# A mixture-of-experts stage with the token lists and gathers first, two tensors for its sums, and its overflow branch moved to the front

## The chip, the cores and the metric

The kernel runs as one program on one core of a Trainium2 chip. The metric is the device time of one execution in microseconds (us), the median of several runs. Engines are named as the profile names them: PE (TensorE products, and PEld its weight loads), DVE (VectorE), ACT (ScalarE), POOL (GpSimd), SP (SyncE); a "q" behind a name is that engine's own queue (branches, waits, DMA issues).

## The reference

Two transformer blocks of two layers each run over 512 tokens of width 1024. Each layer of the first block ends in a hierarchical mixture of experts, and this stage is what the change touches; it occurs twice in the program.

```python
glog = einsum('bsd,dg->bsg', x, wg) + bg                 # 4 groups
gp, gi = top_k(softmax(glog), 1)                         # one group for each token
elog = (the 4 expert logits of that group)
ep, ei = top_k(softmax(elog), 2); ep = ep / sum(ep)      # two experts of that group
combine = sum(one_hot(gi * 4 + ei, 16) * (gp * ep))      # [512, 16], two entries a row
h = silu(x @ w_gate[e]) * (x @ w_up[e]) * combine[:, e]  # 16 experts, 1024 -> 256
ffn = sum over e of h @ w_down[e]                        # 256 -> 1024
x = layernorm(ALPHA * x + ffn)
```

A token's two experts always lie in one group of four (experts 0 to 3, 4 to 7, 8 to 11, 12 to 15), so each expert has 512 x 2 / 16 = 64 tokens on average.

## The kernel before

Matrices are float32 in the interface. On the chip each operand is split into a high and a low float16 part (ACT writes the high part at L133 or L143, DVE the low part at L134 or L144), and each product is three float16 products (`mm3`, L146 to L151).

**Tokens to experts.** `moe` (L1128) first makes the router logits (`rlog`) on PE. DVE then picks the group and the two experts (`first_max`), computes the combination weights `cmb`, and from a triangular product (`pos`, L1186) each token's place in its expert's list. An expert has `CAP` = 104 places. `onehots(e0)` (L1208) makes the one-hot matrices of two experts, eight DVE operations; `select` (L1217) makes expert 0's features with 64 products from the rows that are still in SBUF (the four `xrow` tiles, which fill all four buffers of the pool `xg`); `slots` (L1284) multiplies the one-hots with `V` (token number, three parts of the weight, a one) and so gets for each place the token number, whether it is used, and its weight `cw`. For the other experts an indirect DMA on POOL's queue (`gather`, L1316) fetches all 104 rows, 4 KB each, from the DRAM tensor `rows`, an empty place fetching row 0; `feats` (L1303) transposes them on PE, and ACT copies them out (L1312).

**The loop over experts** (L1353) is written out. In round e PE's order is the features of expert e + 2, the first half of `front(e + 1)` (24 groups of gate and up products, L149 to L151, tile `gu`), the two transposes of expert e (`hT`, L1436), the second half of `front(e + 1)`, and `back(e)`, the down products (tile `ey`). For experts 0 to 13, `back` copies the result out (`yt`, L1329, three buffers) and adds it to the DRAM tensor `res` with an accumulating indirect DMA on POOL's queue (L1332) in which places beyond the list are dropped. All 14 of these scatters write the one tensor `res`, so each waits until the one before has landed. The last two experts keep their results in SBUF and are summed by PE (`ysum`, L1398).

**Weights.** An expert's weights are three chunks of 1 MB (gate and up in two halves, down), 48 chunks in a layer. SP issues their loads (L122) into five staging buffers, so the load of chunk c waits for the split of chunk c - 5. `fetch(n)` splits up to chunk n; the split parts go round 12 pairs of buffers, two of which are the former `xT` tiles. Before the loop `fetch` reaches 9; in round 0 it reaches 10, in round e it reaches 3(e + 3) + 1.

**Overflow.** `overflow` (L1448) handles tokens beyond an expert's 104 places. Every engine loads the count `oi` into a register (L1453) and jumps over the body when it is zero (L1454), as it is for these inputs. The body is a loop over experts with the four token tiles written out. It stands in round 14, behind `back(14)` and ahead of `back(15)`.

**The end.** At the end of round 13 four DMAs on POOL's queue read `res` back (`mx`, L1383), after the last scatter has landed. Then each token tile gets its sum on PE (`ysum`, L1398 and L1400) and its layer norm.

## Time and profile before

| | before |
|---|---|
| median of 3 runs | 2452.76 us (2444.24 to 2454.18) |
| the profiled execution | 2442.73 us |
| its span in the trace | 2441.0 us |
| PE, DVE, ACT, POOL busy in the span | 91%, 70%, 47%, 11% |
| the first expert stage, from the router to the sums | about 316 to 536 us |
| the second expert stage | about 843 to 1081 us |

What lies around the span is 1.7 us. Busy PE time in the profile is modelled: two products that overlap in the pipeline both count. In a timeline row the first number is the start, the second the time to the end of the group (xN is how many), and the bracket tells how long the engine had been idle and what the profile takes for the releaser. A wait for several semaphores is put down to the one that came last; where the engine named had long been done it was another, often a DMA.

### The profile page before, as it was taken

Reading aid. Unit: us, or ns where it says so; the run is one execution under the profiler, and the core shown is the slowest. Engines: PE = TensorE matmul, PEld = TensorE weight load, DVE = VectorE, ACT = ScalarE, POOL = GpSimd, SP = SyncE. Lnnn points to the kernel's source line nnn. Section 1 sums busy time; section 2 is a strip of 40 time slices with the busy share of each in tenths; the row PEclk is TensorE's granted clock in tenths of the full one; section 3 lists DMA queues with packets and bytes.
Section 4 is the critical chain, followed back from the end, with each engine's and each line's share of the span. In section 5 each row is a group of like instructions: output and inputs, shape, how many; then the busy total and the mean of one; then the engine's idle time right before and its main releaser. Section 6 shows DMA issues by size and latency. Waiting matters only on the chain.

```text
span 2441.0 us, 34718 instructions
## 1 busy us (share of the span) xinstructions
PE 2218.6 (91%) x13330; PEld 1210.9 (50%) x13334; DVE 1698.7 (70%) x3668; ACT 1149.9 (47%) x1965; POOL 269.9 (11%) x335
## 2 busy tenths in 40 slices
PE   8888969888889878869998899999999989999999
PEld 4545545544546455535455554444444556544444
DVE  7978878778978868768999654442469996544421
ACT  5546637845546547724545443222245455332320
POOL 1221022221310122211100100000000000000000
PEclk9999979999999989979998999999999999999999
DMA  5311559953311659933212242222331112422222
GB/s 184 122 62 43 181 177 310 339 188 105 115 59 61 242 179 335 309 125 120 74 48 81 71 168 104 104 104 80 130 123 61 61 54 83 167 104 104 104 78 78
DMA packets 58976, 319.45 MB, mean 131 GB/s; under 512 B 9908, under 2 KB 10164, under 8 KB 30384
## 3 DMA queue, kind: packets, MB, share of 16 engines
q1 hardware_dynamic: 40448, 263.67, 30.5%
q0 software_dynamic: 13744, 36.68, 5.7%
q10 hardware_dynamic: 4608, 16.78, 1.8%
q8 instruction: 108, 1.77, 0.3%
q14 instruction: 68, 0.56, 0.1%
HBM read 286.59 MB, written 30.90 MB: 130 GB/s over the span
## 4 chain that ended last, share of the span: by engine, by line
PE 39%; DVE 10%; ACT 4%; issue 2%; DMA 1%; DVEq 0%; ACTq 0%
PE fd L149 3%; PE fd L150 3%; PE fd L151 3%; PE fu L151 3%; PE fg L151 3%; PE fu L150 3%; PE fg L150 3%; PE fu L149 3%; PE fg L149 3%; PE o L795 2%; DVE wl L134 1%; PE gqk L149 1%; PE gqk L151 1%; PE gqk L150 1%; DVE mx L1801 1%
## 5 line engine op out<-in xcount | busy, mean ns | idle before, releaser
L134 DVE SCALAR_TENSOR_TENSOR wl<-wst,wh 128x1024 f16<-128x1024 f32 (+1 forms) x428 | 513.3, 1226 | 205.2 <-ACT wh L133 201.2
L133 ACT ACTIVATE wh<-wst 128x1024 f16<-128x1024 f32 (+1 forms) x428 | 430.2, 1047 | 278.0 <-PE fd L151 107.1
L150 PEld LDWEIGHTS <-wh 128*128 128x128 f16 x968 | 95.4, 99 | 101.9 <-issue 3.8
L151 PEld LDWEIGHTS <-wl 128*128 128x128 f16 x968 | 95.7, 99 | 100.8 <-issue 2.2
L149 PEld LDWEIGHTS <-wh 128*128 128x128 f16 x968 | 95.7, 99 | 99.5 <-issue 2.1
L149 PE MATMUL fd<-wh,fhh 128*128 128x512 f16 x352 | 133.4, 379 | 0.0
L150 PE MATMUL fd<-wl,fhh 128*128 128x512 f16 x352 | 133.4, 379 | 0.0
L151 PE MATMUL fd<-wh,fhl 128*128 128x512 f16 x352 | 133.4, 379 | 0.0
L149 PE MATMUL gqk<-wh,xTh 128*128 128x512 f16 x320 | 122.7, 384 | 7.6 <-ACT rsq L1685 7.3
L151 PE MATMUL gqk<-wh,xTl 128*128 128x512 f16 x320 | 122.7, 384 | 0.0
L150 PE MATMUL gqk<-wl,xTh 128*128 128x512 f16 x320 | 122.6, 383 | 0.0
L149 PE MATMUL fg<-xTh,wh 128*128 128x512 f16 x320 | 121.3, 379 | 0.0
L150 PE MATMUL fg<-xTl,wh 128*128 128x512 f16 x320 | 121.3, 379 | 0.0
L151 PE MATMUL fg<-xTh,wl 128*128 128x512 f16 x320 | 121.3, 379 | 0.0
L149 PE MATMUL fu<-xTh,wh 128*128 128x512 f16 x320 | 121.3, 379 | 0.0
L150 PE MATMUL fu<-xTl,wh 128*128 128x512 f16 x320 | 121.3, 379 | 0.0
L151 PE MATMUL fu<-xTh,wl 128*128 128x512 f16 x320 | 121.3, 379 | 0.0
L150 PEld LDWEIGHTS <-xTh 128*128 128x128 f16 x768 | 74.9, 99 | 71.6 <-issue 13.1
L149 PEld LDWEIGHTS <-xTh 128*128 128x128 f16 x768 | 74.9, 99 | 67.8 <-ACT xTh L143 5.2
L151 PEld LDWEIGHTS <-xTl 128*128 128x128 f16 x768 | 74.3, 99 | 65.9 <-DVE xTl L144 4.6
L1860 DVE SCALAR_TENSOR_TENSOR fth<-fth,fg 128x512 f32<-128x512 f32 x40 | 27.5, 687 | 107.5 <-ACT fth L1859 107.5
L149 PE MATMUL gO<-wh,mTh 128*128 128x512 f16 x256 | 97.7, 383 | 1.5 <-ACT mTh L143 1.4
(615 smaller groups left out, 5471.1 us busy)
## 6 DMA issues: line engine op xcount, KB each, us to landing
wst<-in_w_gu SPq DMA_DIRECT2D x108, 1024.0 KB, 6.5
wst<-in_w_dn SPq DMA_DIRECT2D x52, 1024.0 KB, 4.8
wst<-in_w SPq DMA_DIRECT2D x28, 1024.0 KB, 4.9
wst<-in_wB SPq DMA_DIRECT2D x16, 1024.0 KB, 4.9
wst<-in_w_out SPq DMA_DIRECT2D x16, 1024.0 KB
dk<-d_nc SPq DMA_DIRECT2D x16, 512.0 KB, 3.6
res<-xa SPq DMA_DIRECT2D x8, 512.0 KB
rows<-xrow SPq DMA_DIRECT2D x8, 512.0 KB
```

The lines of the kernel that those rows point to most:

```text
L133: nc.scalar.activation(wh[:, a:b], st[:, a:b], AF.Copy, scale=scale)
L134: (eng or nc.vector).scalar_tensor_tensor(wl[:, a:b], st[:, a:b], scale, wh[:, a:b], op0=ALU.mult, op1=ALU.subtract)
L149: mm(out, ah, bh, start=start, stop=False)
L150: mm(out, ah, bl, start=False, stop=False)
L151: mm(out, al, bh, start=False, stop=stop)
L795: mm(out, p[:, bs], v, start=first, stop=last)
L1801: nc.vector.tensor_reduce(mr[:, t, h:h + 1], ps[:, :n], axis=AX.X, op=ALU.max)
L1860: nc.vector.scalar_tensor_tensor(th, th, 1.0, pg, op0=ALU.add, op1=ALU.mult)
```

## The change

The program computes the same function. The parts, in the order of the diff:

1. **Two tensors for the sums.** `res` becomes two DRAM tensors, both set to the residual by `finish` (four more 512 KB writes a layer on SP's queue). Experts are taken in the order `ORD` = 0, 8, 1, 9, ..., 7, 15, so that even rounds (groups 0 and 1) add to `res[0]` and odd rounds to `res[1]`. Reading back, an indirect DMA takes for each token the row of the tensor that its group went to: eight DMAs in place of four, each with the other tensor's tokens out of bounds.
2. **Lists and gathers first.** `pos` is made by one operation, the one-hots follow at once, and `slots` needs only the token number. An empty place gets an index of 1024, and the gather has a bounds check. The gather of expert 1 goes to a zeroed buffer of its own instead of to the pool that holds `xrow`. Combination weights, `V` and the overflow count come behind the gathers of experts 1 to 3.
3. **Weights split sooner.** `fetch` reaches 9 ahead of the combination weights, 10 ahead of the loop, 12 and 13 in round 0, 15 in round 1, 17 in round 2, and from round 3 on what it reached before. The features of expert 2 come behind `front(1)` instead of ahead of it.
4. **The branch.** `overflow` stands ahead of `front(0)`. Its body is a loop over experts and in it a loop over token tiles, with room in the two `xT` tiles, and it adds to both sum tensors.

```diff
+ORD = [8 * (i % 2) + i // 2 for i in range(NEXP)]
...
+            nx["res"] = [self.drg.tile([T, D], F32, name="res%d" % i, bufs=1) for i in range(2)]
...
-            nc.sync.dma_start(nx["res"][t * P:(t + 1) * P], xa)
+            for r in nx["res"]:
+                nc.sync.dma_start(r[t * P:(t + 1) * P], xa)
...
+            xg1 = m2.tile([P, 2 * D], F16, tag="yt", name="xg1", bufs=self.YT)[:CAP]
+            nc.gpsimd.memset(xg1, 0.0)
...
-            nc.vector.tensor_copy(pos, ps[:, :NT * NEXP].rearrange("p (t e) -> p t e", t=NT))
-            inb = mp.tile([P, NT, NEXP], F32, name="inb")
-            nc.vector.scalar_tensor_tensor(inb, pos, float(CAP), msk, op0=ALU.is_lt, op1=ALU.mult)
+            nc.vector.scalar_tensor_tensor(pos, ps[:, :NT * NEXP].rearrange("p (t e) -> p t e", t=NT), 1.0, mskh,
+                                           op0=ALU.add, op1=ALU.mult)
...
-            nc.vector.scalar_tensor_tensor(posm, pos, 1.0, inb, op0=ALU.add, op1=ALU.mult)
-            nc.vector.tensor_scalar(posm, posm, -1.0, None, op0=ALU.add)
...
+                    nc.vector.scalar_tensor_tensor(midx[:, i], hi[:, :, 0], (2048.0, -2048.0)[i], self.tokf[:, i],
+                                                   op0=ALU.mult, op1=ALU.add)
...
-                        nc.tensor.matmul(ps[:CAP, 5 * e:5 * e + 5], ohs[:, t, e], V[:, t, e0 + e],
+                        nc.tensor.matmul(ps[:CAP, e:e + 1], ohs[:, t, e], self.tokh[:, t:t + 1],
                                          start=t == 0, stop=t == 3)
...
+                nc.vector.tensor_scalar(sidx[:CAP, eg], ps[:CAP, :2], 1024.0, None, op0=ALU.add)
...
-                                             in_offset=bass.IndirectOffsetOnAxis(ap=sidx[:CAP, 0, e:e + 1], axis=0))
+                                             in_offset=bass.IndirectOffsetOnAxis(ap=sidx[:CAP, e:e + 1], axis=0),
+                                             bounds_check=T - 1, oob_is_err=False)
...
-                    nc.gpsimd.indirect_dma_start(out=cur["res"], in_=yt, in_offset=None,
-                                                 out_offset=bass.IndirectOffsetOnAxis(ap=sidx[:CAP, 1, e:e + 1], axis=0),
+                    nc.gpsimd.indirect_dma_start(out=cur["res"][e % 2], in_=yt, in_offset=None,
+                                                 out_offset=bass.IndirectOffsetOnAxis(ap=sidx[:CAP, e:e + 1], axis=0),
                                                  bounds_check=T - 1, oob_is_err=False, compute_op=ALU.add)
...
-            last = slots(0, ohs)
             xgs = {}
-            gather(1)
-            slots(2, onehots(2))
-            ps = [p for p in front(0, xt[0])][0]
-            with tc.issue_after(last.ins):
-                fetch(9)
+            xo = [m2.tile([P, KD, P], F16, tag="xgt%d" % i, name="xgo%d" % i) for i in range(2)]
+            ohs = onehots(0)
+            slots(0, ohs)
+            gather(1)
+            xt = [select(ohs, 0)]
+            oh2 = onehots(2)
+            slots(2, oh2)
             gather(2)
             gather(3)
+            fetch(9)
+            weights()
+            beyond()
+            slot_weights(0, ohs)
+            self.tap("cmb%d" % l, cmb)
+            self.overflow(l, m2, oi, cov, xr_d, xo, feats, cur["res"])
+            ps = [p for p in front(0, xt[0])][0]
+            fetch(10)
+            slot_weights(2, oh2)
+            oh4 = onehots(4)
+            slots(4, oh4)
+            slot_weights(4, oh4)
             xt.append(feats(xgs[1]))
-            slots(4, onehots(4))
             ys, mx = [], []
-            fetch(9)
...
-                if e + 2 < NEXP:
+                if 0 < e < NEXP - 2:
                     xt.append(feats(xgs[e + 2]))
...
+                if e == 0:
+                    xt.append(feats(xgs[2]))
+                    fetch(12)
...
-                    fetch(3 * (e + 3) + 1 if e else 10)
-                if e == NEXP - 2:
-                    self.overflow(l, m2, oi, cov, xr_d, feats, mx)
+                    fetch(max(3 * (e + 3) + 1, 13 + 2 * e))
...
-                        x = self.xg.tile([P, D], F32, tag="xg", name="mx")
-                        nc.gpsimd.dma_start(x, cur["res"][t * P:(t + 1) * P])
-                        mx.append(x)
+                        mx.append(self.xg.tile([P, D], F32, tag="xg", name="mx"))
+                    for i in range(2):
+                        for t in range(NT):
+                            nc.gpsimd.indirect_dma_start(out=mx[t], out_offset=None, in_=cur["res"][i],
+                                                         in_offset=bass.IndirectOffsetOnAxis(ap=midx[:, i, t:t + 1], axis=0),
+                                                         bounds_check=T - 1, oob_is_err=False)
...
-                for t, x in enumerate(sums):
+                with tc.For_i(0, NT, 1) as t:
...
+                    for q in sums:
+                        nc.gpsimd.indirect_dma_start(out=q, in_=y, in_offset=None,
+                                                     out_offset=bass.IndirectOffsetOnAxis(ap=ti, axis=0),
+                                                     compute_op=ALU.add)
```

## Rows read from the trace of the kernel before

**Rows 1.** First stage by stretch: PE, PEld, DVE, ACT, POOL, clock, DMA, GB/s

```profile
350.00:360.00 10.00, 6.51 (x41) 4.42 (x39) 2.28 (x17) 3.13 (x4) 1.95 (x2) 0.52 0.76 172
360.00:380.00 20.00, 19.54 (x126) 12.24 (x125) 13.66 (x30) 14.19 (x20) 5.90 (x4) 1.00 0.58 178
...
440.00:460.00 20.00, 15.73 (x99) 9.54 (x98) 15.44 (x27) 15.97 (x22) 4.37 (x3) 1.00 1.01 338
```

**Rows 2.** DMA queues from 410 to 490 us: packets, MB, share of 16 engines

```profile
q1 hardware_dynamic: 3171, 23.10, 80.1%
q0 software_dynamic: 1677, 4.08, 20.6%
```

**Rows 3.** Start times of expert transposes on PE, first stage, then second stage

```profile
360.34 0.34 PE L1436 MATMUL hT<-idf,eth 104*128 104x104 f32 x2
369.39 0.34 PE L1436 MATMUL hT<-idf,eth 104*128 104x104 f32 x2
...
499.18 0.34 PE L1436 MATMUL hT<-idf,eth 104*128 104x104 f32 x2
...
886.92 0.34 PE L1436 MATMUL hT<-idf,eth 104*128 104x104 f32 x2
...
1023.86 0.34 PE L1436 MATMUL hT<-idf,eth 104*128 104x104 f32 x2
```

**Rows 4.** POOL's timeline: first gather, last scatters and read-backs of each stage

```profile
342.64 1.72 POOL L1319 DMA_INDIRECT xg<-rows,sidx  x1 [11.31 <-DVE cwt L1299]
...
504.15 2.47 POOL L1332 DMA_INDIRECT res<-yt,sidx  x1 [3.95 <-ACT yt L1329]
514.23 1.63 POOL L1332 DMA_INDIRECT res<-yt,sidx  x1 [7.61 <-ACT y L143]
520.86 2.27 POOL L1383 DMA_DIRECT2D mx<-res  x4 [5.00 <-DMA res<-yt,sidx]
...
1031.31 1.68 POOL L1332 DMA_INDIRECT res<-yt,sidx  x1 [3.66 <-ACT yt L1329]
1044.89 2.66 POOL L1332 DMA_INDIRECT res<-yt,sidx  x1 [11.90 <-ACT wh L133]
1055.95 2.24 POOL L1383 DMA_DIRECT2D mx<-res  x4 [8.41 <-DMA res<-yt,sidx]
```

**Rows 5.** Timeline of ACT and PE: expert 13 copied out, first product with `mx`

```profile
504.92 0.62 ACT L1329 ACTIVATE yt<-ey 104x512 f32<-104x512 f32 x1
...
527.08 2.08 PE L1400 MATMUL ysum<-mx,ida 128*128 128x512 f32 x2 [4.15 <-DMA mx<-res]
...
1029.95 0.63 ACT L1329 ACTIVATE yt<-ey 104x512 f32<-104x512 f32 x1
...
1059.89 2.07 PE L1400 MATMUL ysum<-mx,ida 128*128 128x512 f32 x2 [9.18 <-DMA mx<-res]
```

**Rows 6.** Timeline of DVE at the head of the first stage: one-hots, indices

```profile
335.74 0.39 DVE L1213 TENSOR_SCALAR ohs<-iota_h,posm 128x104 f16<-128x104 f16 x2
...
341.45 0.16 DVE L1294 CAST sidx<-sl 104x2 int32<-104x2 f32 x1
```

**Rows 7.** Timeline of PE at the head of the first stage

```profile
340.43 0.90 PE L1290 MATMUL slots<-V,ohs 128*104 128x5 f16 x16
...
354.58 0.87 PE L1309 MATMUL xgT<-idh,xg 104*128 104x104 f16 x8 [3.49 <-DMA xg<-rows,sidx]
355.25 0.63 PE L149 MATMUL gu<-wh,xgt 128*104 128x512 f16 x1
```

**Rows 8.** SP's queue: loads of weight chunks 13, 14, and 15 with 16

```profile
344.74 0.34 SPq L122 DMA_DIRECT2D wst<-in_w_gu  x1
364.43 0.33 SPq L122 DMA_DIRECT2D wst<-in_w_dn  x1
373.48 2.60 SPq L122 DMA_DIRECT2D wst<-in_w_gu  x2
```

**Rows 9.** The jump over the overflow body, line L1454: min/median/max ns, both stages

```profile
L1454 PEldq COMPARE_BRANCH  x2: 4003/4870/5737, 512.6 to 1037.8; - x2
...
L1454 DVEq COMPARE_BRANCH  x2: 63/68/72, 514.7 to 1040.1; - x2
```

189 lines of the change are left out of this document (105 added, 84 removed).

## The prediction

> **What bounds the kernel now.** I read the busy time by stretch first, because the share over the whole span says nothing of two stages that make up about a fifth of it. In the expert stage PE is starved at the head, with about half its clock granted (0.52, the 1.2 GHz level) from 350 to 360 us, and then loses a fifth of its time in the loop, 15.73 of 20 us busy from 440 to 460 us, while the DMA engines stand at a share of 1.01 [rows 1]. At the head they are not full: 0.76 from 350 to 360 us and 0.58 from 360 to 380 us [rows 1].
>
> Next, the DMA queues inside the full stretch, to price the loop. From 410 to 490 us the weights move 23.10 MB in 80.1% of the engines [rows 2]. A chunk is 1.0486 MB, so these are 22.0 chunks or 7.34 experts, 10.9 us each; a chunk costs 0.801 x 80 / 22.0 = 2.91 us of all engines. Gathers and scatters take the other 20.6%, 16.5 us for 4.08 MB, or 248 GB/s [rows 2].
>
> Third, the expert transposes as a clock of the loop. Rounds 0 to 13 take 499.18 - 360.34 = 138.8 us in the first stage and 1023.86 - 886.92 = 136.9 us in the second, 10.7 and 10.5 us a round; the first round, before the DMA engines fill up, takes 9.05 us [rows 3]. So PE could go at about 9 us and the DMA engines hold it at 10.5 to 11.
>
> Last, the end. Expert 13's result is ready at 504.92 + 0.62 = 505.5 us [rows 5], but its scatter is issued at 514.23 [rows 4]. The profile names ACT as its releaser; that work was long done, and what ended just then is the scatter of 504.15 before it, 10.1 us earlier, on the same tensor [rows 4]. In the second stage the result is ready at 1030.6 [rows 5] and goes out at 1044.89, 13.6 us behind the scatter of 1031.31 [rows 4]. Then the read-back waits for that landing, 6.6 and 11.1 us [rows 4], and PE's first product with `mx` comes at 527.08 and 1059.89, after idle times of 4.15 and 9.18 us [rows 5]. Counted from the transposes of expert 13 [rows 3] that is 27.9 and 36.0 us.
>
> **Head, part 2 and part 4.** One-hots start at 335.74 and the indices come at 341.45 [rows 6], because `select`, casts and `V` lie between. In the new order the eight one-hots follow `pos` directly, with two mask operations and one subtraction fewer: I put the start 0.9 us sooner, the eight at about 0.2 us each (two in 0.39 [rows 6]), then the small products and one cast, so indices at about 337. The first gather then goes out at about 337.5 instead of 342.64 [rows 4], and no longer waits for `select` to free a buffer of `xg`. The rows it reads have left by then or nearly so; if not, it loses 1 to 2 of these 5 us.
>
> Against this, `front(0)` now stands behind everything that feeds the branch. Before, it followed `slots` at 340.43 + 0.9 [rows 7]. Now PE must first take the count product, the weight products of experts 0 and 1 (with DVE's weight chain, some 25 small operations of 0.16 us and more [rows 6], partly under `select`) and the jump. Before, PE's jump took 4.0 and 5.7 us, and DVE's 0.06 to 0.07 [rows 9]. PE's body had four tiles of 16 + 24 + 2 + 12 products, each with its weight load, 432 instructions; now it is one tile, 108. No row has a jump over 108, so I bound it between DVE's and PE's price, 0.07 to 5.7 us, and take 2. The Trainium skill, "Runtime: NRT & Kernel Launch", section "Instruction fetch mechanics", says that a taken branch stalls only where its target is outside the pages fetched ahead; by that the short body may cost next to nothing, and the sum would gain 2 us a stage more, while at PE's old price it would lose 2 to 4.
>
> `front(0)` is thus some 4 us later (1 to 10). But what bounded the first rounds was the second gather: features of expert 2 waited for it until 354.58 and `front(1)` stood behind them at 355.25, at half clock [rows 1, 7]. Now they stand behind `front(1)`. With `front(0)` over at about 351 and the features of expert 1 made at 354, the transposes of expert 0 come at about 358 instead of 360.34 [rows 3]: **a gain of 2 us a stage**, from +6 (no stall, full clock) to -4 (stall, half clock).
>
> **Loop, parts 2 and 3.** A gather fetched 104 rows and now fetches 64 on average: 40 x 4 KB = 0.164 MB less, 0.66 us at 248 GB/s or 0.45 us at the weights' 361 GB/s [rows 2]. Over the nine or so full rounds that is 4 to 6 us. A price of zero needs the dropped rows to cost as much as real ones, which I keep as the lower end.
>
> The load of a chunk waits for the split of the fifth before it. Chunk 13 left at 344.74, 14 at 364.43, 15 with 16 from 373.48 [rows 8], though staging was what kept them, the DMA engines being 0.58 busy [rows 1]. Splits 9 to 12 now come in or before round 0, so chunks 14 to 17 leave some 10 us sooner; the lead shrinks to nothing in the emitted order by round 3, and only what was moved in idle time stays: at most 0.24 x 10 + 0.42 x 20 = 10.8 us [rows 1]. I take half, 5 us, of which PE can use 3, since it can't go below 9.05 a round [rows 3]. **Loop: 8 us a stage**, from 0 to 14 (13 rounds at 9.6 us, half a microsecond above PE's best round).
>
> The Trainium skill, "DMA: Bandwidth & Descriptors", section "Issuing engines are not separate DMA queues", says that all transfers share the same 16 engines whoever issues them; this speaks against part 1 inside the loop, where the trace agrees (share 1.01), and two chains of scatters there buy nothing by themselves. I give them nothing in the loop.
>
> **Tail, parts 1 and 4.** With two tensors, scatter 13 waits only for scatter 11, which is long down, and goes out as soon as `yt` is ready, 6.7 us after the transposes. It lands 6.6 to 10.1 us later in the first stage [rows 4], at +13.3 to +16.8. The four reads of `res[0]` run on POOL meanwhile. Reads of `res[1]` follow; from read-back to PE's product it was 6.2 us (520.86 to 527.08) [rows 4, 5], and an indirect DMA takes up to 1 us longer to issue (1.63 to 2.47 against 2.27 for four direct ones [rows 4]). That is +20 to +24.5 where it was +27.9: **5.5 us**, from 3 to 8. In the second stage landing takes 11.1 to 13.6 us, as the next mixer's weights load at the same time, and read-back to product 3.9 us [rows 4, 5]: +22 to +25 where it was +36.0: **12 us**, from 8 to 14. PE's jump of 4.0 and 5.7 us [rows 9] leaves the end and costs nothing there any more; it lay beside the same wait, so I don't count it again.
>
> **Costs.** Four more residual writes a layer are 2.1 MB, about 6 us of the DMA engines, ahead of the stage. SP issues them, and loads of chunks stand behind them; five chunks are already staged there, so I cost this at 0, and at 1.5 us, one write, if the gather waits for it. Eight indirect reads take POOL 8 to 13 us against 2.27 [rows 4]; half lie under the scatter's landing and the others are consumed one token tile at a time: 0, at worst 3 us a stage. POOL's next work, the following mixer's parameters, moves back by as much but forward with the stage.
>
> **Sum.** 2 x (2 + 8) + 5.5 + 12 = 37.5 us. Against the profiled execution, 2442.73 us, that gives 2405.2; the median of the runs lies 10.0 us above it, so the forecast is 2452.8 - 37.5 = **2415 us**. All good ends together give 62 us (2 x 20 + 22), all bad ones 2 x (-4 + 0 - 3) + 11 = -3.
>
> **Rivals.** *The DMA engines hide the head start.* If dropped rows cost like real ones and the splits only move waiting from one buffer to another, the loop gains nothing. For it: a share of 1.01 through the loop [rows 1]. Against: idle share at the head. Then only the tail remains, 11 to 17.5 us less a little: 2438 to 2445 us, say 2441.
>
> *The branch becomes the gate at the head, and the kernel gets slower.* Place: PE's queue ahead of `front(0)`, with ACT, DVE and POOL behind the same jump. Price: a jump at the old mean of 4.87 us [rows 9], about 3 us for the weight chain, and `front(0)` at half clock, its 24 of a round's 36 wide products being at most 6.0 of 9.05 us [rows 3], so 6 us more: 14 us, less 5 for the earlier gather, 9 later a stage. With nothing from the loop, the bad end of the tail (11) and 3 us a stage for the reads, that is 2 x 12 - 11 = +13: 2466 us. It decides from the point where the transposes of expert 0 come more than 17.5 / 2 = 8.8 us later than at 360.34 and the loop doesn't give it back. Against it: the body is a quarter as long.
>
> *The scatters still go one by one* (the change doesn't do what it says), because something else on POOL's queue orders them. Then the tail keeps its waits and only 2 x 10 us come: 2433 us. Against: idle POOL ahead of each scatter [rows 4].
>
> **How the numbers follow.** Forecast 0.70, hidden head start 0.18, gate 0.08, one by one 0.04. A measurement of this kernel tells about 0.5%, 12 us, from no change; the second case straddles that line, 0.07 faster and 0.11 the same. Faster 0.81, same 0.11, slower 0.08. The range reaches from all good ends, 2391, to 2452, where the bad ends stop and the gate begins.
>
> **What would show it.** Indices at about 337 and a first gather before 339; PE's jump under 2 us and expert 0's transposes at 355 to 362; chunks 14 to 16 loaded before 365; rounds of 9.7 to 10.4 us; scatter 13 within 8 us of its transposes, overlapping scatter 12; first product with `mx` at +20 to +25 in both stages. The forecast is wrong if the loop keeps its 10.6 us a round, if the clock stays at half through `front(0)`, or if the reads back leave PE idle as long as before.

## The result, and the profile after

The changed kernel takes **2428.95 us** (median of 4 runs, 2427.74 to 2434.0) against 2450.26 us of the kernel before on the same chip (2444.24 to 2454.18): a ratio of 0.9921, with a 95% interval from 0.9901 to 0.994. It is faster, by 21 us where 37.5 were forecast. The profiled execution of the kernel after took 2429.33 us, the one of before 2442.73 us, so the two traces hold 13.4 us of the difference, and these can be followed to their places.

Five times serve as a clock in every kernel below: the router's logits (`lg` on VectorE), the transposes of experts 0 and 13 (`hT` on PE), the first product with `mx`, and the first product of the next mixer. The head is the stretch from the logits to expert 0, the loop from expert 0 to expert 13, the tail from expert 13 to `mx`.

The logits come first, from VectorE's timeline of the kernel before. Columns of a timeline: start in us, duration in us, engine, line, operation, output and inputs, shapes, count, and in brackets the idle time ahead of it and what ended it.

```profile
328.93 0.24 DVE L1143 SCALAR_TENSOR_TENSOR lg<-rlog,rb 128x80 f32<-128x80 f32 x1 [0.53 <-PE rlog L151]
```

The same timeline of the kernel after, from the last layer norm ahead of the router on:

```profile
318.98 1.17 DVE L136 SCALAR_TENSOR_TENSOR wl<-wst,wh 128x1024 f16<-128x1024 f32 x1
...
325.90 1.22 DVE L136 SCALAR_TENSOR_TENSOR wl<-wst,wh 128x1024 f16<-128x1024 f32 x1
...
332.40 0.24 DVE L1158 SCALAR_TENSOR_TENSOR lg<-rlog,rb 128x80 f32<-128x80 f32 x1 [0.53 <-PE rlog L153]
...
339.81 1.65 DVE L1245 TENSOR_SCALAR ohs<-iota,pos 128x104 f16<-128x104 f16 x10
341.48 0.16 DVE L1307 TENSOR_SCALAR sidx<-slots 104x2 int32<-104x2 f32 x1
```

The router is 3.5 us later than before: four halves of weight splits, 4.8 us (two of the rows are shown), now stand between the layer norm's small steps. From that norm's last statistics (`ln_st`) to the logits it takes 15.5 us, before 12.4. The indices come at 341.48, as before [rows 6], although the one-hots stand ahead of `select` now: the weight chain (`cmb`, `V`, `cov`), which the code lists behind them, still runs ahead of them.

PE's transposes in the kernel after, those of experts 0 and 13 in stage 1, then in stage 2; they answer to [rows 3]:

```profile
356.61 0.35 PE L1476 MATMUL hT<-idf,eth 104*128 104x104 f32 x2
...
492.17 0.40 PE L1476 MATMUL hT<-idf,eth 104*128 104x104 f32 x2 [0.64 <-DVE eth L1473]
...
878.47 0.34 PE L1476 MATMUL hT<-idf,eth 104*128 104x104 f32 x2
...
1014.04 0.40 PE L1476 MATMUL hT<-idf,eth 104*128 104x104 f32 x2 [2.86 <-DVE eth L1473]
```

Expert 0 is 3.7 and 8.5 us sooner than before, and measured from the logits 7.2 and 7.5 us sooner. Expert 13 is 7.0 and 9.8 us sooner, so by the transposes the loop has gained 3.3 and 1.4 us.

But expert 13's transposes do not stand at the same place of PE's order in the two kernels. The gate and up products (`gu`, 24 for each expert) from the logits to these transposes, first of the kernel before, then of the kernel after (stretch, its length, PE's busy time in these products and their number, clock, DMA share, GB/s):

```profile
328.93:499.18 170.25, 80.77 (x348) 0.90 0.85 277
```

```profile
332.40:492.17 159.77, 82.41 (x360) 0.93 0.87 285
```

In the kernel after, 12 products more are done by then, which take PE 2.6 us. Expert 0's transposes stand behind 36 products in both. From the 36th product to the 360th it takes 141.6 and 139.7 us before, 134.8 and 132.5 us after: by equal work the loop has gained 6.8 and 7.2 us.

The jump over the overflow body, columns as in [rows 9]:

```profile
L1497 PEldq COMPARE_BRANCH  x2: 228/284/339, 346.5 to 868.2; - x2
```

It costs 0.23 to 0.34 us on PE, where it took 4.0 to 5.7 us [rows 9]. The Trainium skill, "Runtime: NRT & Kernel Launch", section "Instruction fetch mechanics", says that a taken branch stalls where its target lies outside the pages at hand. Both prices agree with that; whether the old target lay outside and the new one does not, no run here shows.

Busy time by stretch in stage 1, columns as in [rows 1]:

```profile
350.00:360.00 10.00, 9.91 (x90) 6.93 (x90) 9.18 (x23) 8.03 (x12) 4.08 (x2) 1.00 0.60 195
360.00:380.00 20.00, 20.00 (x135) 12.84 (x133) 13.81 (x35) 15.55 (x23) 5.48 (x4) 1.00 0.81 245
440.00:460.00 20.00, 14.70 (x70) 8.49 (x68) 13.96 (x21) 13.58 (x20) 4.84 (x4) 0.83 0.95 311
```

The clock at expert 0 is the full 2.4 GHz level (1.00) where it was 0.52 [rows 1], and the DMA engines are busier from 360 to 380 us, 0.81 against 0.58. From 440 us on PE starves as before.

GpSimd's timeline at the end of stage 1, answering to [rows 4]: the last two scatters (L1354) and the reads of the two sums (L1422).

```profile
486.85 2.00 POOL L1354 DMA_INDIRECT res<-yt,sidx  x1 [2.94 <-ACT yt L1351]
496.56 2.07 POOL L1422 DMA_INDIRECT mx<-res,midx  x1 [7.71 <-DMA res<-yt,sidx]
...
503.94 1.64 POOL L1354 DMA_INDIRECT res<-yt,sidx  x1 [0.31 <-issue]
511.42 1.04 POOL L1422 DMA_INDIRECT mx<-res,midx  x1 [5.83 <-issue]
```

Scatter 13 (503.94) does not go out when its rows are ready (499.3). Four reads of the even sum stand ahead of it, and the first of them waits 7.71 us (11.90 in stage 2) for scatter 12's landing. ACT's timeline at the same place shows a second wait, one that the prediction does not list:

```profile
493.91 1.06 ACT L226 ACTIVATE lnb<-lnb 128x1024 f32<-128x1024 f32 x1 [2.76 <-DMA lnb<-in_ln_b]
494.87 0.37 ACT L1471 ACTIVATE eth<-gu 104x256 f32<-104x256 f32 x1
495.13 0.34 ACT L145 ACTIVATE ehh<-hT 128x208 f16<-128x208 f32 x1
```

ACT waits for a row of the next layer norm, whose first use on VectorE is at 527.5 us, and the split of expert 13's hidden values (`ehh`, whose transposes ended at 492.6) stands behind it. The Trainium skill, "PSUM — Partial Sum Buffer", section "Engine vs sequencer instructions", says that ScalarE's, VectorE's and GpSimd's queues are strictly first in, first out; both rows agree, with 2.76 and 7.71 us. The end of it, on PE, answering to [rows 5]:

```profile
518.95 2.08 PE L1440 MATMUL ysum<-mx,ida 128*128 128x512 f32 x2 [4.98 <-DMA mx<-res,midx]
...
1042.74 2.07 PE L1440 MATMUL ysum<-mx,ida 128*128 128x512 f32 x2 [4.23 <-DMA mx<-res,midx]
```

That is 26.8 and 28.7 us behind expert 13's transposes (before, 27.9 and 36.0). Counted from the 360th product it is 27.8 and 31.9 us (before, 25.3 and 33.5), so by equal work the tail has gained nothing over both stages.

### The profile page after: what moved, and what is told of

The parts are those of the page before. It is cut to its first block, busy times and chain, and to the rows that moved or that the text cites. A ratio compares the mean times of both kernels' runs of the same rounds, so it can differ in the third digit from the quotient of the medians.

```text
span 2427.6 us, 34940 instructions
## 1 busy us (share of the span) xinstructions
PE 2218.0 (91%) x13462; PEld 1215.2 (50%) x13462; DVE 1690.5 (70%) x3602; ACT 1148.7 (47%) x1965; POOL 288.9 (12%) x345
## 4 chain that ended last, share of the span: by engine, by line
PE 41%; DVE 10%; issue 5%; ACT 5%; DMA 3%; POOL 1%; POOLq 0%; ACTq 0%; DVEq 0%
PE fd L151 3%; PE fd L153 3%; PE fd L152 3%; PE fg L152 3%; PE fu L152 3%; PE fg L153 3%; PE fu L153 3%; PE fg L151 3%; PE fu L151 3%; PE o L800 2%; DMA res<-yt,sidx 2%; DVE wl L136 1%; PE gqk L151 1%; PE gqk L152 1%; PE gqk L153 1%
## 5 line engine op out<-in xcount | busy, mean ns | idle before, releaser
L152 PEld LDWEIGHTS <-xTh 128*128 128x128 f16 x768 | 75.0, 99 | 73.9 <-issue 15.6
```

The source lines that it names most:

```text
L152: mm(out, ah, bl, start=False, stop=False)
```

## The experiments

The kernel before was run again beside each kernel, on the same chip (medians of 2448.2 to 2450.6 us). The table gives the ratio to it and, from each trace, the head, the loop and the tail as defined above, stage 1 / stage 2, in us. The last column is the loop by equal work, from the 36th to the 360th product. The transposes of experts 0 and 13 stand behind 36 and 360 products in every kernel but the one before (36 and 348), `no_branch` (24 and 360), `old_splits` (24 and 348), `sf_ln_ahead` (36 and 348) and `sf_ln_pin2` (48 and 360); for these five, head, loop and tail can't be compared with the others row by row.

| kernel | ratio (95%) | median | head | loop | tail | 36th to 360th |
|---|---|---|---|---|---|---|
| before | 1 | 2450.26 | 31.4 / 31.6 | 138.8 / 136.9 | 27.9 / 36.0 | 141.6 / 139.7 |
| after | 0.9921 (0.9901-0.994) | 2428.95 | 24.2 / 24.1 | 135.6 / 135.6 | 26.8 / 28.7 | 134.8 / 132.5 |
| pin | 0.9954 (0.9933-0.9975) | 2438.59 | 25.5 / 32.3 | 134.8 / 135.2 | 28.0 / 32.6 | 133.9 / 134.6 |
| scatter_first | 0.9901 (0.9879-0.9924) | 2426.27 | 24.1 / 24.1 | 135.9 / 135.6 | 26.6 / 24.6 | 135.0 / 132.7 |
| one_tensor | 0.9911 (0.989-0.9933) | 2427.61 | 23.4 / 23.5 | 133.3 / 133.5 | 31.4 / 27.6 | 132.5 / 132.7 |
| no_branch | 0.9931 (0.9911-0.9952) | 2433.60 | 23.6 / 23.4 | 140.0 / 139.6 | 28.5 / 30.1 | 135.5 / 133.2 |
| ln_late | 0.9909 (0.9882-0.9935) | 2426.38 | 25.2 / 24.5 | 134.2 / 136.0 | 25.7 / 25.9 | 133.4 / 135.2 |
| sf_ln | 0.9857 (0.9829-0.9885) | 2416.29 | 24.0 / 24.0 | 135.6 / 135.5 | 23.2 / 20.2 | 134.7 / 132.8 |
| one_tensor_ln | 0.9904 (0.9878-0.993) | 2424.37 | 23.0 / 22.2 | 132.3 / 132.6 | 31.3 / 25.1 | 131.4 / 131.1 |
| full_gather | 0.9938 (0.9916-0.9961) | 2435.60 | 25.1 / 24.5 | 137.5 / 137.6 | 27.8 / 28.6 | 136.7 / 134.4 |
| old_splits | 1.0 (0.9987-1.0013) | 2449.38 | 21.1 / 21.1 | 143.6 / 144.5 | 27.3 / 29.6 | 142.8 / 143.6 |
| sf_ln_ahead | 0.9941 (0.9923-0.9958) | 2435.96 | 24.1 / 23.9 | 140.0 / 141.4 | 24.1 / 23.9 | 142.8 / 144.2 |
| sf_ln_pin2 | 0.9861 (0.9841-0.9881) | 2417.22 | 30.4 / 29.7 | 135.1 / 131.8 | 23.6 / 20.3 | 139.3 / 136.0 |
| sf_ln_wr | 0.9853 (0.9831-0.9875) | 2412.99 | 23.3 / 23.2 | 136.3 / 134.7 | 23.1 / 20.4 | 135.4 / 133.3 |

My theory after the first look: the head's mechanism held, but the splits that were let go take it back ahead of the router; the tail is held by the order on GpSimd's queue. The rivals: the second write of the residual rows holds the router; the landings hold the tail; the tensors or the branch cost or bring something else than forecast.

### The router: pin

```diff
-            fetch(9)
+            with tc.issue_after(last.ins):      # last: the sidx step of slots(0)
+                fetch(9)
...
-            fetch(10)
+            with tc.issue_after(last.ins):
+                fetch(10)
```

> The changed kernel with the splits of chunks 8 and 9 held on VectorE behind the list of expert 0 (the first list's `sidx`), as the kernel before held chunk 8's; nothing else is moved. Theory A: the router came 3.5 us late in the changed kernel (logits `lg` at 332.40 against 328.93) because four split halves of 1.2 us slid in between the layer-norm steps ahead of it; then the logits come back to 328.9 +- 0.7 in stage 1 and some 3.5 us sooner in stage 2, and the time is 2419 to 2424 us. Rival B: the second write of the residual rows on SP, or the traffic of the loads that leave sooner, holds the router up; then the logits stay at 332 +- 0.7 and the time at 2427 to 2431. Rival C: the router comes back but the four halves are paid again ahead of expert 0's middle, so that expert 0's transposes stay at 356.6 +- 0.7 and the time at 2427 to 2431.

The time came out 10 us above the kernel after, against theory A's 2419 to 2424. In stage 2 the router did come back: from the next mixer's first product to the logits it is 318.6 us instead of 323.1 (before, 316.5). In stage 1 the logits stand at 333.65; this execution was already 4.9 us behind the kernel before at about 200 us, ahead of anything that the edit touches. Measured inside the norm, from its last statistics to the logits, it takes 12.4 us there, as before, and 8.5 us in stage 2 against 12.5 in the kernel after. The four halves are thus what delayed the router, by 3.0 and 4.0 us. In the head they cost 1.3 us in stage 1 and 8.2 us in stage 2. VectorE's timeline in stage 2:

```profile
862.02 2.35 DVE L136 SCALAR_TENSOR_TENSOR wl<-wst,wh 128x1024 f16<-128x1024 f32 x2
...
864.79 0.15 DVE L1307 TENSOR_SCALAR sidx<-slots 104x2 int32<-104x2 f32 x1
...
865.18 1.22 DVE L136 SCALAR_TENSOR_TENSOR wl<-wst,wh 128x1024 f16<-128x1024 f32 x1
```

Held behind the first list, the halves run ahead of the second list (864.79); so they do in stage 1. In stage 2 PE then waits twice, for a small step of VectorE and for the landing of a gather, from PE's timeline:

```profile
873.94 0.77 PE L1317 MATMUL slotw<-V,ohs 128*104 128x3 f16 x8 [2.25 <-DVE sl L1320]
...
878.00 0.70 PE L1331 MATMUL xgT<-idh,xg 104*128 104x104 f16 x6 [2.36 <-DMA xg<-rows,sidx]
```

Its clock falls with it; the stretch from 870 to 880 us in this kernel, then in the kernel after:

```profile
870.00:880.00 10.00, 5.39 (x53) 3.76 (x52) 6.11 (x14) 5.67 (x7) 5.09 (x2) 0.67 0.75 224
```

```profile
870.00:880.00 10.00, 9.63 (x82) 6.44 (x81) 7.25 (x21) 6.94 (x9) 4.46 (x3) 1.00 0.56 168
```

PE is busy 5.39 of these 10 us and the granted clock is 0.67 in the mean, between the two levels; the head takes 32.3 us instead of 24.1. The tails are longer too, by 1.2 and 3.9 us. Rival C is nearest, at a higher price than it named; why stage 2 pays it and stage 1 does not is open.

### The tail: scatter_first, ln_late and both together (sf_ln)

The first edit holds all reads of the sums behind scatter 13, the second holds ACT's scaling of the norm's row behind expert 15's split, `sf_ln` makes both:

```diff
+                    with tc.issue_after(sc.ins):       # sc: the scatter of expert 13
                         for i in range(2):
                             for t in range(NT):
                                 nc.gpsimd.indirect_dma_start(out=mx[t], ...)
...
+            with tc.issue_after(h[2][0]):              # ACT's split of expert 15
+                g, b = self.ln_rows(self.ew[1], "ln2", l, nx["kind"], 1.0 / AS, "wh")
```

> The changed kernel with all eight reads of the two sums held on GpSimd behind the scatter of expert 13; nothing else is moved. Theory A: the order on GpSimd's queue costs the tail its gain, because the four reads of the even sum wait there for scatter 12's landing (7.71 us idle in stage 1, 11.90 in stage 2) with scatter 13 queued behind them. Then scatter 13 leaves 6 to 8 us after expert 13's transposes (in the changed kernel 11.8 and 13.2), and the first product on `mx` comes 21 to 24 us after them (26.8 and 28.7): the four issues of the even sum, some 7.4 us, still stand ahead of the odd sum's. 3 to 6 us each stage, time 2417 to 2423. Rival B: the landing of the scatters and the weight loads beside them set the tail; then the first product on `mx` stays within 1 us of 26.8 and 28.7 and the time at 2427 to 2431.

Half of theory A: the tail fell to 24.6 us in stage 2, but stayed at 26.6 in stage 1, and the time at 2426. Scatter 13 left 9.1 and 9.9 us after its transposes, not 6 to 8, since its rows themselves were late, behind the wait on ACT that is shown above.

> The changed kernel with ACT's scaling of the next layer norm's row (`lnb` in stage 1, `lng` in stage 2) held behind the split of expert 15's hidden values; nothing else is moved. In the changed kernel ACT waited 2.76 and 3.23 us for that row's landing with the split of expert 13's hidden values queued behind it. Theory A: that wait lies on the path of experts 13 to 15; expert 15's transposes come 12.5 to 14 us after expert 13's instead of 15.6 and 15.5, but the first product on `mx` still waits for scatter 13 behind the reads of the even sum, so it stays 25 to 29 us after expert 13's transposes and the time at 2423 to 2429 us. Rival B: PE is held at the end by the last chunks' loads and splits; then expert 15's transposes stay within 0.7 us of where they stood.

As theory A has it: expert 15's transposes come 13.0 and 10.2 us after expert 13's (15.6 and 15.5 before the edit), the tail is 25.7 and 25.9 us, the time 2426.

> The kernel with the reads behind scatter 13, and ACT's scaling of the next norm's row behind expert 15's split. Theory A: the order on GpSimd and the row on ACT cover each other; with both gone scatter 13 leaves 6 to 7.5 us after expert 13's transposes (9.1 and 9.9 with the reads alone moved), the first product on `mx` comes 20.5 to 23.5 us after them, and the time is 2414 to 2422. Rival B: the last chunks or the reads themselves hold the end: the first product stays 24 us or more after them, time 2423 to 2429.

Both moves bring 12.7 us, where each alone brought under 3 in the medians, which the intervals can't tell from nothing; in the tails of both stages it is 12.1 us against 4.3 and 3.9. They cover each other, as theory A said. GpSimd's timeline of `sf_ln` in stage 2, and PE's first product on `mx` there:

```profile
1012.03 1.96 POOL L1354 DMA_INDIRECT res<-yt,sidx  x1 [10.06 <-ACT yt L1351]
1014.30 1.08 POOL L1423 DMA_INDIRECT mx<-res,midx  x1 [0.30 <-issue]
...
1022.44 0.99 POOL L1423 DMA_INDIRECT mx<-res,midx  x1 [3.02 <-DMA mx<-res,midx]
```

```profile
1027.24 1.12 PE L1442 MATMUL ysum<-mx,ida 128*128 128x512 f32 x2 [0.53 <-DMA mx<-res,midx]
```

Scatter 13 leaves 5.0 us after its transposes, the reads of the even sum run under its landing, and PE waits 0.53 us instead of 4.23. The tail is 23.2 and 20.2 us, inside the 20 to 25 that the prediction gave it.

### Two tensors or one: one_tensor, one_tensor_ln

```diff
-            nx["res"] = [self.drg.tile([T, D], F32, name="res%d" % i, bufs=1) for i in range(2)]
+            nx["res"] = [self.drg.tile([T, D], F32, name="res0", bufs=1)]
...
-                    nc.gpsimd.indirect_dma_start(out=cur["res"][e % 2], in_=yt, in_offset=None,
+                    nc.gpsimd.indirect_dma_start(out=cur["res"][0], in_=yt, in_offset=None,
...
-                            (the eight indirect reads)
+                    for t in range(NT):
+                        nc.gpsimd.dma_start(mx[t], cur["res"][0][t * P:(t + 1) * P])
```

> The changed kernel with one tensor for the sums again: one write of the residual rows, all scatters to one tensor, plain reads of it. Theory A: the gains of the loop (3.3 and 1.4 us up to expert 13's transposes) and of the tail (1.1 and 7.3 us) come from the two tensors. Then expert 13's transposes lie 138 to 139 us after expert 0's (135.6 in the changed kernel) and the first product on `mx` 28 to 36 us after them, time 2438 to 2444. Rival B: the loop's gain comes from the splits that were let go sooner, and only the tail is lost: expert 13's transposes stay 135 to 136.5 us after expert 0's, time 2430 to 2438. Rival C: one tensor is the better now, since its reads are half as many and none is indirect, and the router has one write less ahead of it: time 2420 to 2428.

The time is that of the kernel after, as rival C allows: the tail is longer in stage 1 (31.4 us), but the loop is shorter by 2.3 and 2.1 us (by products, 2.3 and nothing), which no theory had. The wait on ACT was at its worst here, 9.85 us, from ACT's timeline of this kernel:

```profile
497.27 1.06 ACT L226 ACTIVATE lnb<-lnb 128x1024 f32<-128x1024 f32 x1 [9.85 <-DMA lnb<-in_ln_b]
```

So the comparison was made again with that wait gone (the `ln_rows` edit on top):

> The kernel with one tensor, and ACT's scaling of the next norm's row behind expert 15's split (that wait was 9.85 and 7.81 us with one tensor). Theory A: two tensors are worth something at the end once ACT no longer covers it: with one tensor scatter 13 still waits for the landing of scatter 12, so the first product on `mx` comes 25 to 29 us after expert 13's transposes, 3 to 7 us behind the kernel with two tensors, both moves made; time 2419 to 2427. Rival B: they are worth nothing, since the second write, the eight reads and the small packets cost what the wait did: the time is within 2 us of that kernel or below it.

Against `sf_ln` the tail is 8.0 and 4.9 us longer, as theory A said, the loop 3.3 and 2.9 us shorter (by products 3.3 and 1.7) and the head 1.0 and 1.8. The medians are 8.1 us apart. Two tensors are worth something, but by less than the tail shows, because the loop pays for them. In stage 1 ACT still waits, now for a weight chunk of the next mixer, and PE stands 8.36 us ahead of expert 15's transposes:

```profile
502.60 1.06 ACT L135 ACTIVATE wh<-wst 128x1024 f16<-128x1024 f32 x1 [9.01 <-DMA wst<-in_wA]
```

In `sf_ln` this wait is 2.38 us. What ends last is still the sums: the last scatter stands 10.39 us on GpSimd for the landing of the one before, and PE waits 2.83 us for `mx`. Stage 2, where expert 15 comes 10.2 us behind expert 13 in both kernels, is the clean comparison.

### What the loop pays: sf_ln_wr

The second residual write makes SP hold chunk 14's load: SP's timeline of `sf_ln`, where the writes of the last token tile stand ahead of it:

```profile
334.97 1.21 SPq L285 DMA_DIRECT2D res<-xa  x2
336.27 1.14 SPq L124 DMA_DIRECT2D wst<-in_w_dn  x1
```

```diff
-            for r in nx["res"]:
-                nc.sync.dma_start(r[t * P:(t + 1) * P], xa)
+            for r, q in zip(nx["res"], (nc.sync, nc.gpsimd)):
+                q.dma_start(r[t * P:(t + 1) * P], xa)
```

> The kernel with both tail moves, and the second write of the residual rows issued by GpSimd instead of SP; SP's order of loads and writes is then that of the kernel with one tensor, the bytes stay. In the kernel with both tail moves the load of chunk 14 stood on SP behind the last token tile's three writes and left at 336.27 us against 326.62 with one tensor. Theory A: that place on SP's queue is what two tensors cost (expert 13's transposes 135.5 us after expert 0's against 132.3 and 132.6); then chunk 14 leaves near 326, that distance falls to 132 to 133.5 in both stages, and the time to 2407 to 2413 us. Rival B: the bytes of the second write, 2.1 MB a stage, or the scatters running two at a time cost it; then the distance stays 135 to 136 and the time 2414 to 2419. Rival C: four more issues on GpSimd delay the first gather; expert 0's transposes come over 1 us later against the logits than 24.0.

Chunk 14 did leave at 326.75, and the head gained 0.7 to 0.8 us, but the loop stayed at 136.3 and 134.7: theory A falls on the cause, and rival B stands, though the time, 2412.99, lies at the edge of theory A's band (2407 to 2413) and not in rival B's (2414 to 2419). The DMA queues from 400 to 440 us (packets, MB, share of 16 engines), first of `sf_ln_wr`, then of `one_tensor_ln`, show which half of it:

```profile
q1 hardware_dynamic: 1518, 11.04, 78.2%
q0 software_dynamic: 1129, 1.96, 21.4%
```

```profile
q1 hardware_dynamic: 1617, 11.77, 81.2%
q0 software_dynamic: 927, 1.55, 17.4%
```

The second write is long over there. With two tensors 4 scatters and 5 gathers are issued in these 40 us, the scatters 9.3 to 11.0 us apart; with one tensor 4 and 4, the scatters 10.1 to 13.2 us apart, each held by the landing of the one before. What waits on GpSimd leaves the engines to the weights: 0.73 MB more, or 0.7 chunk, some 2 us at 2.9 us a chunk [rows 2]. Two tensors let the scatters take their share just where the weights are short. That this is all of the 3 us is worked out, not shown by an edit of its own.

### The branch: no_branch

```diff
-            self.overflow(l, m2, oi, cov, xr_d, xo, feats, cur["res"])
```

> The changed kernel without the overflow branch: its count, jump, loop and the two tiles that its body keeps are left out, so tokens beyond an expert's capacity would go uncorrected. Theory A: the jump ahead of expert 0's products is nearly free (0.23 to 0.34 us on the engines): expert 0's transposes come within 1 us of where they stand against the router's logits (24.2 us after them in both stages), time 2426 to 2431. Rival B: the branch as a boundary holds work up (two splits waited 9.6 us behind it, no instruction may cross it): expert 0's transposes 3 to 6 us sooner against the logits, time 2416 to 2424.

By the transposes theory A has the price: the head is 23.6 and 23.4 us instead of 24.2 and 24.1. But they stand behind 24 products here instead of 36. The 36th product comes 27.0 and 26.8 us after the logits instead of 24.0 and 23.9, and the median is 5 us above the kernel after (the intervals of the two ratios overlap), because the branch does something else. Its body keeps the two buffers of chunks 10 and 11 until the jump. Without it VectorE takes those splits ahead of the lists, from its timeline:

```profile
335.64 1.22 DVE L136 SCALAR_TENSOR_TENSOR wx<-wst,wx 128x1024 f16<-128x1024 f32 x1
...
340.25 1.22 DVE L136 SCALAR_TENSOR_TENSOR wx<-wst,wx 128x1024 f16<-128x1024 f32 x1
...
343.33 0.16 DVE L1307 TENSOR_SCALAR sidx<-slots 104x2 int32<-104x2 f32 x1
```

Four halves stand between the router and the first list, which comes 11.6 us after the logits instead of 9.1; the first gather goes out at 344.44, and the first product of `front(0)` comes 15.8 us after the logits instead of 13.4.

### The dropped rows: full_gather

```diff
+                nc.vector.tensor_scalar(gidx[:CAP, eg], ps[:CAP, :2], 1024.0, T - 1.0, op0=ALU.add, op1=ALU.min)
...
-                                             in_offset=bass.IndirectOffsetOnAxis(ap=sidx[:CAP, e:e + 1], axis=0),
+                                             in_offset=bass.IndirectOffsetOnAxis(ap=gidx[:CAP, e:e + 1], axis=0),
```

> The changed kernel with the empty places of the gathers filled again: their index is cut to the last row, so that all 104 rows are fetched as in the kernel before; one more small VectorE step of 0.15 us a pair; the scatters still drop. Theory A: what the dropped rows leave out is 0.164 MB a gather, 0.45 to 0.66 us of a full set of DMA engines, and the full stretch holds 8 to 10 gathers: the last chunk's load leaves 4 to 6 us later in each stage and the time is 2436 to 2444. Rival B: a dropped row costs as much as a fetched one (one small packet of it is left): last load and time within 2 us of the changed kernel, 2427 to 2431. Rival C: less load early only moves waiting, part of it comes back: 2431 to 2436.

The loop is 2.0 us longer in both stages (1.9 by products), the time 2435.6, in the band of rival C. Of the 7.6 us between the profiled executions (spans 2435.2 and 2427.6) 3.5 lie ahead of stage 1's router, which the edit does not touch. GpSimd's queue over the whole of stage 1, from the logits to the first product on `mx` (packets, MB, share of 16 engines), of this kernel in 190.4 us and then of the kernel after in 186.6 us:

```profile
q0 software_dynamic: 5406, 12.67, 26.3%
```

```profile
q0 software_dynamic: 5636, 10.67, 22.9%
```

The packets are not fewer: a dropped row still leaves a small one. Its bytes are gone, 2.0 MB (2.2 in stage 2), which are 7.4 and 9.5 us of all engines over the 15 gathers of a stage, or 0.5 to 0.6 us a gather. 2.0 us of them reach PE; where the others stay was not traced.

### The splits: old_splits and sf_ln_ahead

```diff
-                    fetch(12)
...
-                    fetch(max(3 * (e + 3) + 1, 13 + 2 * e))
+                    fetch(3 * (e + 3) + 1 if e else 10)
```

> The changed kernel with the splits inside the loop let go where the kernel before let them go (chunk 9 at expert 0, then up to chunk 3 x (e + 3) at expert e; the changed kernel goes to chunks 12, 14 and 16 at experts 0, 1 and 2). Theory A: these splits are what fills the DMA engines from 360 to 400 us; without them the share there falls from 0.81 and 0.92, the last chunk's load leaves 3 to 6 us later, expert 13's transposes come 138 to 140 us after expert 0's, time 2433 to 2441. Rival B: the loop is bound by the DMA engines from 400 us on and gives the head start back; within 1 us of 135.6 and 2427 to 2431.

This undoes a few chunk numbers in three rounds, and takes back the whole gain: ratio 1.0. By the transposes the loop is 8.0 and 8.9 us longer and the head 3.1 and 3.0 us shorter; but they stand behind 24 and 348 products here. By products the head is 0.5 and 0.7 us longer and the loop 8.0 and 11.1 us, and from the logits to the product on `mx` it takes 5.4 and 6.8 us more. Theory A has the right place and half the price. By the profiled executions the span is 11.6 us longer (2439.2 against 2427.6); this kernel's lies at the low end of its runs, 2440.97 to 2457.37. Busy time in two stretches of this kernel, then in the later one of the kernel after (its earlier one is shown above):

```profile
360.00:380.00 20.00, 19.54 (x141) 12.58 (x140) 11.19 (x24) 14.37 (x21) 6.10 (x4) 1.00 0.44 126
...
420.00:440.00 20.00, 16.75 (x103) 10.87 (x104) 13.90 (x20) 14.07 (x20) 4.29 (x3) 0.75 0.93 302
```

```profile
420.00:440.00 20.00, 19.89 (x132) 12.41 (x131) 14.90 (x22) 15.64 (x23) 7.45 (x5) 1.00 1.00 329
```

The early splits free staging buffers, the DMA engines go from 0.44 to 0.81, and PE stays fed until 440 us instead of 400. So the next step seemed plain, one expert further ahead, on top of `sf_ln`:

```diff
-                    fetch(max(3 * (e + 3) + 1, 13 + 2 * e))
+                    fetch(max(3 * (e + 4) + 1, 13 + 2 * e))
```

> The kernel with both tail moves, and the splits in the loop let go one expert further ahead (up to chunk 3 x (e + 4) at expert e). Theory A: the DMA engines still have 0.19 and 0.08 of 20 us to give from 360 to 400 us, 5.4 us; if half of it reaches the end, expert 13's transposes come 132 to 134 us after expert 0's and the time is 2409 to 2414. Rival B: the added splits on ACT and VectorE stand ahead of the experts' own steps there; the first rounds go from 9.3 to 10 us or more, and the time is 2415 to 2421.

It loses 20 us against `sf_ln`. The rounds take 10.2 to 10.4 us from the second on, as rival B has it, but only because 28 products instead of 24 stand between two transposes there: the 132nd product comes 61.4 us after the logits, in `sf_ln` 60.5. By the 216th it is 100.2 against 91.5, and the cause is one that neither theory had. ACT's timeline of this kernel, and PE's:

```profile
413.06 1.06 ACT L135 ACTIVATE wh<-wst 128x1024 f16<-128x1024 f32 x1 [2.71 <-DMA wst<-in_w_dn]
...
417.62 2.00 ACT L135 ACTIVATE wh<-wst 128x1024 f16<-128x1024 f32 x2 [1.59 <-DMA wst<-in_w_gu]
...
421.00 0.67 ACT L1473 ACTIVATE eth<-gu 104x256 f32<-104x256 f32 x2
```

```profile
422.43 0.61 PE L1478 MATMUL hT<-idf,eth 104*128 104x104 f32 x2 [5.43 <-DVE eth L1475]
```

ACT has reached chunks that have not landed, waits for them 2.71 and 1.59 us, and the expert's own step (`eth`) stands behind; PE idles 5.43 us for it. A split that is let go too early turns from a help to the loads into a wait on ACT.

### The router again: sf_ln_pin2

```diff
-            fetch(9)
...
-            fetch(10)
-            slot_weights(2, oh2)
+            lw = slot_weights(2, oh2)
+            with tc.issue_after(lw.ins):
+                fetch(10)
```

> The kernel with both tail moves, and the splits of chunks 8 and 9 held on VectorE behind the weights of experts 2 and 3, that is behind the second list too (the first pin stood behind the first list only). Theory A: the router comes some 3 us sooner in both stages and expert 0's transposes stay 23.5 to 25 us after the logits; time 2408 to 2412. Rival B: the four halves, 4.9 us, now stand ahead of expert 0's middle step, and the loads of chunks 13 and 14 that wait for them leave 15 us later: expert 0's transposes come 27 us or more after the logits, and the time is 2415 to 2422.

Rival B. VectorE's timeline has the four halves right ahead of expert 0's middle step:

```profile
354.65 4.62 DVE L136 SCALAR_TENSOR_TENSOR wl<-wst,wh 128x1024 f16<-128x1024 f32 x4
359.19 0.16 DVE L1319 TENSOR_SCALAR sl<-slotw 104x6 f32<-104x6 f32 x1
359.27 0.42 DVE L1474 SCALAR_TENSOR_TENSOR eth<-eth,gu 104x256 f32<-104x256 f32 x1
```

The head goes to 30.4 and 29.7 us by the transposes, which stand behind 48 products here; by the 60th product, where the orders agree again, it is 2.6 and 2.0 us longer. The router gives 3.0 and 4.0 us back, the loop behind it is longer, and the time is that of `sf_ln`. Neither pin found a place for these 4.8 us between the layer norm and expert 0 that made the kernel faster.

The best kernel is thus `sf_ln_wr`, 2412.99 us and 0.9853 of the kernel before, 0.7% below the changed kernel; `sf_ln` can't be told from it by the ratios.

## Why the prediction was right and wrong

The direction was right, and the size was about 0.57 of the forecast by the medians (21.3 of 37.5 us). Term by term, both stages together, from the two traces:

| term | forecast | measured |
|---|---|---|
| head, from the logits | 4 | 14.7 (7.2 + 7.5) |
| loop, to expert 13; by the 360th product | 16 | 4.7 (3.3 + 1.4); 14.0 (6.8 + 7.2) |
| tail, from there to the product on `mx` | 17.5 | 8.4 (1.1 + 7.3); -0.9 (-2.5 + 1.6) |
| from there to the next mixer | 0 | -0.5 |
| ahead of the two routers | 0 | -10.1 (3.5 + 6.6) |
| block two | 0 | -3.8 |
| sum | 37.5 | 13.4 |

**Head.** The mechanism was right and the gain more than the 2 us a stage, for two reasons. PE's jump took 0.3 us and not 2. And the clock did better than the middle that I took: `front(0)` begins at 345.8, about where the forecast put it although the router was late, and the stretch up to the transposes runs at the full level. One checkpoint of the head failed: indices at 337 and the first gather before 339 did not come (341.48 and 342.62). Of these 4.5 us the later router is 3.5; the rest is the weight chain, for which the forecast took the order of the code for the order on VectorE. The head gained without it.

**Ahead of the router.** This is the step that is missing in the prediction. It lists where splits come sooner and costs them in idle time, but names no queue that they are moved past. The old code held two of the halves behind the first list and made the other two in round 0; let go, all four stand on VectorE ahead of the router, and they cost it 3.0 us in stage 1 and 4.0 in stage 2, by `pin`. `sf_ln_pin2` has the same 12.4 and 8.5 us. The edits that moved them a few steps did not have this price back: `pin` pays 1.3 and 8.2 us in the head, `sf_ln_pin2` 2.6 and 2.0 by the 60th product and more in the loop. The other 2.6 us ahead of stage 2's router were not traced. The 3.8 us of block two stay open as well. From the next mixer's first product to the end it takes 1358 us before and 1362 after, and in the other kernels 1358 to 1369 although none changes anything there.

**Loop.** The prediction took the transposes for the clock of the loop, and the change moved that clock by 12 products. By them the loop gained 4.7 us of 16, by equal work 14.0. That this is near the forecast is in part luck, for none of its parts has the size it was given. Dropped rows brought 1.9 to 2.0 us a stage against 4 to 6: the price of a gather was right, 0.5 to 0.6 us of all engines against 0.45 to 0.66, and the step that failed is that PE gets all of it. The early splits brought 8.0 and 11.1 us by products against 3: mis-sized to the low side. And the price of part 1 was forgotten. "I give them nothing in the loop" was meant as a zero gain; by the transposes it is a loss of 2 to 3 us a stage, by products of 0 to 3.3. The rule cited there from the Trainium skill ("DMA: Bandwidth & Descriptors", "Issuing engines are not separate DMA queues") agrees with the rows: while the scatters of two tensors moved 1.96 MB with the gathers and not 1.55, the weights moved 11.04 MB and not 11.77. The rival "DMA engines hide the head start" did not come: the load of the last chunk leaves 150.3 and 147.9 us after the logits, before 160.9 in both stages.

**Tail.** This term failed in the changed kernel: scatter 13 left 11.8 and 13.2 us after the transposes and not within 8, the product on `mx` came at +26.8 and +28.7 and not at +20 to +25, and by equal work the tail gained nothing. 20 to 25 us was the right size once the two waits were gone, as `sf_ln` shows, with 4.7 and 15.9 us of gain by the transposes against 5.5 and 12 forecast (1.1 and 10.5 from the 360th product). What failed is the step "goes out as soon as `yt` is ready": the prediction put the four reads of the even sum under scatter 13's landing without asking in which order they stand on GpSimd. They stood ahead of it. The rival "scatters still one by one because something else on POOL's queue orders them" (0.04) named just this for the last pair, and priced it for the whole tail; its 2433 lies nearer to the measured 2429 than the forecast's 2415. The wait on ACT for the norm's row is not in the prediction at all. In the kernel before, that scaling stood at 507.33 us, behind expert 13's copies [rows 5], and waited 0.57 us; in the new order it stands ahead of them. From the 360th product to the stage's last, PE takes 11.8 and 16.8 us after the change (before, 8.3 and 8.7), and 9.3 in both stages of `ln_late`.

**Costs.** Extra writes and reads at 0 held for the reads: in `sf_ln` the odd sum's reads start 10.4 us behind the scatter and PE waits 0.53 us in stage 2. The second write cost 0.7 us a stage in the head, by `sf_ln_wr`, within the 0 to 1.5 given. The gate rival did not come near: with the short body the jump costs 0.3 us.

## What to carry to other kernels

When a hold on an instruction is taken away, follow where the order of its engine puts it next, and cost it there; here 4.8 us of splits moved past the router, and reads moved past a scatter. Before a tail is credited with a transfer that starts sooner, read what stands in front of it on the issuing queue and on every engine that feeds it: two waits that cover each other brought under 3 us one at a time and 12.7 us together. How far ahead work is let go has a price on both sides: of the three settings that were run, less lost 20 us in waits for a free buffer, and more lost 20 us in waits for data on ACT's queue. And before a stage is timed from mark to mark, count the work between the marks: transposes that stood 12 products later made a gain of 14.0 us look like 4.7.

## What the runs showed that was not expected

- A branch that costs 0.3 us was worth 3 us a stage as a hold: its body's two buffers kept four splits of 1.22 us behind the lists.
- Scatters that wait for each other were the better order inside the loop: 11.77 against 11.04 MB of weights in 40 us.
- A dropped row of an indirect read still leaves a packet: 5636 packets against 5406 in stage 1, with 2.0 MB less.
- An indirect read of 128 rows is issued by GpSimd in about 1.0 us (0.99 to 1.12 in most rows of `sf_ln`), half of what its scatters take (1.6 to 2.0): eight of them cost the tail nothing once they stood behind the scatter.
